# Tokens of a tile laid out by residue modulo 16 in a hybrid attention and gating step

## The chip, the core and the metric

The kernel runs on one core of a Trainium2 chip. Its metric is the device time in microseconds of one launch. A core has five instruction queues that run side by side and meet at semaphores: TensorE (PE in the profile; its weight loads are listed apart as PEld), VectorE (DVE), ScalarE (ACT), GpSimd (POOL) and SyncE (SP), which here only starts transfers. Each queue runs its instructions in program order, so an instruction that waits holds up everything behind it on its engine.

## The reference

One decoder step for a prompt of 2048 tokens and a small sample group (8 sequences of 4 tokens). After a norm and one input projection, eight attention heads of 64 channels and a chunked spatial gate run side by side; their outputs are concatenated, projected, added to the input, and followed by a SwiGLU feed-forward and a last norm. The attention is the part that the change is about: every head evaluates three branches with keys at distances 0, d, 2d, ... up to a window, for (window, d) = (128, 1), (512, 4) and (2048, 16), each with its own softmax, and merges them with weights that come from the softmax denominators.

```python
BRANCHES = ((128, 1), (512, 4), (2048, 16))

def _dilated_prompt(q, k, v, bias_hj, d, nj):
    ...
    s = jnp.einsum('bnqrhc,bnkrhc->bnrhqk', qb, kc).astype(jnp.float32)
    s = s * (HEAD_DIM ** -0.5) + bias[None, None, None]
    s = jnp.where(valid[None, :, None, None], s, NEG_INF)
    lse = jax.nn.logsumexp(s, axis=-1)
    p = jnp.exp(s - lse[..., None])
    o = jnp.einsum('bnrhqk,bnkrhc->bnqrhc', p.astype(vc.dtype), vc)
    ...

def _merge_branches(outs, lses):
    w = jax.nn.softmax(jnp.stack(lses, axis=0), axis=0)
    return jnp.sum(w[..., None] * jnp.stack(outs, axis=0).astype(jnp.float32), axis=0)
```

For d = 16 and 2048 tokens the third branch splits the sequence into 16 residue classes of 128 tokens; within a class it is plain causal attention of 128 queries on 128 keys.

## The kernel before

All matmuls take their operands as pairs of a rounded high part and a low remainder, and add two or three products. The launch has three stages: the projections with the gate and the sample attention (to about 607 us of the profile), the attention heads (607 to about 970 us), and the output projection with the feed-forward (the rest). Projected queries, keys and values go through DRAM (`qk_d`, `v_d`), as does a table of attention biases (`b_d`, written by `table_spread`, L483).

A head is a list of 20 *items* (L1081 to L1084): 16 *band* items, one for each tile of 128 queries, which serve the branches (128, 1) and (512, 4) together on up to five tiles of keys; and four *strided* items ("s"), each with four residue classes of the third branch. In the middle heads (list `OTHER`) the strided items stand at places 2, 7, 12 and 17. Head 0 and head 7 have lists of their own.

The order on each engine is written out by hand. `at(step, phase, function)` files a call, and `Plan.run` issues all calls by step, then by phase (L46: early, exp, low, scores, turn, mid, values, out, misc, store), then in the order of filing. An item at step x passes through these steps:

- x: its scores on PE into a PSUM tile `ps_s` (two buffers), phase scores;
- x + 1: DVE adds the bias and finds the minimum (scores are kept negated); for a strided item POOL then subtracts the minimum (L935);
- x + 2 or x + 3: ACT takes the exponential;
- x + 3 (band) or x + 4 (strided): PE transposes the probabilities into PSUM (`ps_a`, three banks in turn) and ACT copies the high parts out (`ph`, `eh`), phase turn;
- x + 4 in phase low (band) or x + 5 in phase mid (strided): DVE subtracts to get the low parts (`pl`, `el`, L896), after which the bank is free;
- later PE multiplies with the values (L910 for a group of four band items, L958 and L959 for a strided item), and ACT copies the result out (L919 and L966).

`strided_scores` (L921) reads query and key columns with a step of 16 (`bass.ds(r4 * 4 + a, P, step=NT)`), 128 of them, one matmul for each of the two query parts and each of four residues. The queries are the stationary operand, the keys the moving one. `strided_out` (L961) writes the 128 outputs of a residue 16 floats apart, so that `o3` lies in token order.

The class `Stats` (L973) makes the merge weights of a head from minima and sums. Band statistics lie as (token in tile, tile), strided ones as (place in class, class). `a` and `b` bring the band statistics to the strided layout with a small DVE product and two small matmuls (L989); `weights_a` and `weights_b` compute the two factors of each token, and `store` writes them to DRAM (`f_d`), from where `merge_load` spreads them over all partitions for the three operations of `merge` (L1031, on POOL in all heads but the last). For the middle heads the steps of `Stats` are filed at steps 2 to 6 of the next head.

`load_head` (L815) brings a head's queries, keys, biases and values on SP's queue; the values come twice, in tile order for the band (`vb`) and in class order for the strided items (`vp`).

Of the kernel before, what the change touches and what calls it, by code (L numbers as in the profile page):

```python
# [10 lines left out]
F32 = mybir.dt.float32  # L11
# [23 lines left out]
BIG = 3.0e38  # L35
SL = 352


# [26 lines left out]
def hymba_step(ctx: ExitStack, tc: tile.TileContext, A: dict, O: dict):  # L65
# [193 lines left out]
    def gate_loads():  # L259

        mask["w"] = big_raw()
        sync.dma_start(mask["w"], A["sgu_wT"])
        mask["c"] = big_raw()[:, 0]
        sync.dma_start(mask["c"], A["causal"])
        sync.dma_start(sgb, A["sgu_bT"])
        sync.dma_start(lng, dap(A["sgu_ln_g"], 0, [[0, P], [1, DA]]))
        sync.dma_start(lnb, dap(A["sgu_ln_b"], 0, [[0, P], [1, DA]]))
        dve.memset(wbd, 0.0)
        sync.dma_start(sgbs, dap(A["sgu_bT"], 0, [[0, SB], [H, ST], [1, H]]))
        sync.dma_start(cms, A["causal_s"])  # L270

    def gate_diagonal(b):
        sync.dma_start(wbd[b * ST:(b + 1) * ST, :, b * ST:(b + 1) * ST], A["sgu_wT"][0:ST, :, 0:ST])

# [540 lines left out]
    def load_head(h):  # L815

        d = heads[h] = {}
        qk = hev if h % 2 == 0 else hod
        for nm, w_, parts in (("qh", 0, (0, 0)), ("k", 1, (0, 1)), ("ql", 0, (1, 1))):
            t_ = d[nm] = qk.tile([P, T], F32R, name=nm, tag="qk", bufs=3)  # L820

            sync.dma_start(t_.bitcast(F32), dap(qk_d, ((w_ * 2 + parts[0]) * DA + h * C) * T,
                                                [[T, C], [(parts[1] - parts[0]) * DA * T, 2], [1, T]]))
            yield
        b_ = row_tile("b")
        d["b3"], d["b12"] = b_[:, 640:768], b_[:, 0:640]
# [9 lines left out]
        sync.dma_start(t_.bitcast(F32), dap(v_d, h * 2 * C, [[NT * H * 2 * C, P], [H * 2 * C, NT], [1, 2 * C]]))  # L836
# [84 lines left out]
    def strided_scores(it):  # L921
        d, st, r4 = it["d"], it["st"], it["n"]
        it["s"] = s = ps_s()[:, 0, :]
        for a in range(4):
            qs = bass.ds(r4 * 4 + a, P, step=NT)
            pe.matmul(s[:, a * P:(a + 1) * P], d["qh"][:, qs], d["k"][:, qs], start=True, stop=False)
            pe.matmul(s[:, a * P:(a + 1) * P], d["ql"][:, qs], d["k"][:, qs], start=False, stop=True)

# [32 lines left out]
    def strided_out(it):  # L961
        r4, h = it["n"], it["h"]
        if r4 == 0:
            o3s[h] = rp.tile([P, P, NT], F32, name="o3", tag="wide", bufs=2)
        rs = slice(r4 * 4, r4 * 4 + 4)
        act.activation(o3s[h][:, :, rs].rearrange("p i r -> p r i"),  # L966
                       it["o"].rearrange("p (r i) -> p r i", r=4), AF.Copy)

# [4 lines left out]
    class Stats:  # L973
        def __init__(self, h, st, r0=0, r1=P):
            self.h, self.st, self.r0, self.r1 = h, st, r0, r1

        def small(self, tag, n):
            return hsmall(tag, n * NT, 2)[0:self.r1].rearrange("p (a t) -> p a t", a=n)

        def a(self):  # L980
            n = self.r1 // 8
            self.m = ap_.tile([P, 2 * P], F32, name="sm", tag="sm", bufs=1).rearrange("p (a n g) -> p a n g", a=2, g=8)[:, :, 0:n]
            dve.tensor_tensor(self.m, self.st["t"][:, 0:2, 0:n].unsqueeze(3).broadcast_to([P, 2, n, 8]),
                              sel_g.unsqueeze(1).unsqueeze(1).broadcast_to([P, 2, n, 8]), op=OP.mult)

        def b(self):
            self.p = pt = ps_a()
            for z in range(2):
                pe.matmul(pt[0:self.r1, z * NT:(z + 1) * NT], self.m[:, z].rearrange("p n g -> p (n g)"), sel_r, start=True, stop=True)  # L989

        def c(self):
            self.s = self.small("s12", 2)
            dve.tensor_copy(self.s.rearrange("p a t -> p (a t)"), self.p[0:self.r1, 0:2 * NT])

        def weights_a(self):

            m3 = self.st["t"][0:self.r1, 2, :]
            self.f = f = self.small("f", 3)
            dve.tensor_tensor(f[:, 2, :], self.s[:, 0, :], m3, op=OP.min)
            dve.tensor_sub(f[:, 0, :], f[:, 2, :], self.s[:, 0, :])  # L1000
            dve.tensor_sub(f[:, 1, :], f[:, 2, :], m3)
            act.activation(f[:, 0:2, :], f[:, 0:2, :], AF.Exp)

        def weights_b(self):
            f, m = self.f, self.f[:, 2, :]
            dd = self.small("dd", 2)
            dve.tensor_mul(dd[:, 0, :], f[:, 0, :], self.s[:, 1, :])
            dve.tensor_mul(dd[:, 1, :], f[:, 1, :], self.st["t"][0:self.r1, 3, :])
            dve.tensor_add(m, dd[:, 0, :], dd[:, 1, :])
            dve.reciprocal(m, m)  # L1010
            dve.tensor_mul(f[:, 0:2, :], f[:, 0:2, :], m.unsqueeze(1).broadcast_to([self.r1, 2, NT]))
# [19 lines left out]
    def merge(h, ch, eng, part=None):  # L1031
        f1, f3 = mf[h, ch]
        x = obs[h][:, ch * 512:(ch + 1) * 512]
        y = o3s[h].rearrange("p i r -> p (i r)")[:, ch * 512:(ch + 1) * 512]
        if part in (None, 0):
# [66 lines left out]
    for y in (222, 224, 226, 228):  # L1102
        at(y, "misc", load, 0)
    at(232, "misc", load, 0)
    at(B0 + 3, "early", load, 0)
    at(B0 + 3, "store", load, 0)
    for h in range(1, H):
# [3 lines left out]
        for y in (1, 2, 3, 4, 10, 12):  # L1111
            at(s0 + y, "misc", load, h)
    def stats_of(h, steps, r0, r1):
        d = {}
        at(*steps[0], lambda: d.update(s=Stats(h, sts[h], r0, r1)))
        for (y, ph), fn in zip(steps, "a b c weights_a weights_b store".split()):
            at(y, ph, lambda fn=fn: getattr(d["s"], fn)())

    for h in range(H):
# [4 lines left out]
        if end:  # L1124

            x = s0 - NI
            stats_of(h, [(x + y, ph) for y, ph in ((14, "early"), (14, "turn"), (15, "early"), (15, "misc"), (16, "early"), (16, "mid"))], 0, 64)
            steps = ((2, "early"), (2, "turn"), (3, "early"), (4, "early"), (5, "early"), (5, "early"))
            at(x + 18, "mid", merge_load, h, 0)
# [5 lines left out]
        else:  # L1135
            steps = ((2, "misc"), (3, "misc"), (4, "early"), (4, "misc"), (5, "misc"), (6, "mid"))

# [7 lines left out]
            else:  # L1145
                at(s0 + 23, "store", merge_store, h, 0, 4)
        stats_of(h, [(s0 + y, ph) for y, ph in steps], 64 if end else 0, P)
    for i, it in enumerate(items):
# [31 lines left out]

    sel_g = ap_.tile([P, 8], F32, name="sel_g", bufs=1)
    sel_r = ap_.tile([P, NT], F32, name="sel_r", bufs=1)
    dve.reduce_sum(sel_g, ident.rearrange("p (g r) -> p g r", g=8), axis=AX.X)
    dve.reduce_sum(sel_r, ident.rearrange("p (g r) -> p r g", g=8), axis=AX.X)

# [741 lines left out]


def _bucket(dist):
    me = 16  # L1930
# [23 lines left out]
def _shape_constants():  # L1954
# [6 lines left out]
    for t in range(ST):  # L1961
# [3 lines left out]
        for u in range(3):  # L1965
# [6 lines left out]
    headmask = np.repeat((rr[:, None] % H == np.arange(H)[None, :]).astype(np.float32), C, axis=1)  # L1972
    sel = ((rr[:, None] % SR) // H == np.arange(ST)[None, :]).astype(np.float32)
    return {"oh12": oh12, "oh3": oh3, "ohs": ohs.reshape(33, 12, P), "causal": causal, "causal_s": causal_s,
            "headmask": headmask, "sel": sel}
# [6 lines left out]
def _arrays(inp):  # L1982
    f = {k: np.asarray(v) for k, v in inp.items()}
    a = {
        "x_prompt": f["x_prompt"].reshape(T, D),
        "x_promptT": f["x_prompt"].reshape(T, D).T,
        "x_sample": f["x_sample"].reshape(SR, D),
# [6 lines left out]
        "sgu_ln_b": f["sgu_ln_b"],  # L1994
        "sgu_wT": f["sgu_w"][0].transpose(2, 0, 1),
        "sgu_bT": f["sgu_b"][0].T,
        "w_out": f["w_out"][0],
# [29 lines left out]
```

## Time and profile before

| | us |
|---|---|
| three runs: lowest, median, highest | 2689.18, 2700.57, 2710.32 |
| the profiled execution: its span, first to last instruction | 2690.7 |
| projections, gate, sample attention | 0 to about 607 |
| attention heads | about 607 to 970 |
| output projection and feed-forward | about 970 to the end |
| HBM over the span | 382.76 MB read, 165.84 MB written |

The profile gives a span, and no time of its own for what lies around it. In the lines that are shown below, a group's line has the source line, engine, operation, output and inputs by the program's names, shapes and count; after the first bar the total busy time in us and the mean of one in ns; after the second bar the idle time of the engine just before them and what ended it. A line of the order of time has the start in us, the duration in us, and the instruction; idle time before it stands in brackets. Matmuls are pipelined, so the durations of neighbours overlap.

### The profile page before, as it was taken

Reading aid. Unit: us, or ns where it says so; the run is one execution under the profiler, and the core shown is the slowest. Engines: PE = TensorE matmul, PEld = TensorE weight load, DVE = VectorE, ACT = ScalarE, POOL = GpSimd, SP = SyncE. Lnnn points to the kernel's source line nnn. Section 1 sums busy time; section 2 is a strip of 40 time slices with the busy share of each in tenths; the row PEclk is TensorE's granted clock in tenths of the full one; section 3 lists DMA queues with packets and bytes.
Section 4 is the critical chain, followed back from the end, with each engine's and each line's share of the span. In section 5 each row is a group of like instructions: output and inputs, shape, how many; then the busy total and the mean of one; then the engine's idle time right before and its main releaser. Section 6 shows DMA issues by size and latency. Waiting matters only on the chain. (4 is left out here: it accounts for less than half of the span.)

```text
span 2690.7 us, 38857 instructions
## 1 busy us (share of the span) xinstructions
PE 2545.5 (95%) x13578; PEld 2245.5 (83%) x13578; DVE 1423.0 (53%) x2884; ACT 1239.5 (46%) x2617; POOL 1322.9 (49%) x968
## 2 busy tenths in 40 slices
PE   8998899998999979899999999899999998999997
PEld 6777677677888867899899987899999987999996
DVE  3258785436788764444444456444444456444445
ACT  6414344446777654545545444523232335433333
POOL 2036663131444354667677653535454533666663
PEclk9999899998999989899999999999999999999998
DMA  7765844586576565345546366445454454555653
GB/s 244 217 200 160 273 138 144 176 268 219 159 238 170 157 166 188 124 150 178 171 157 196 124 191 199 142 140 196 157 178 170 161 176 139 167 202 200 204 194 119
DMA packets 314680, 481.05 MB, mean 179 GB/s; under 512 B 26968, under 2 KB 179721, under 8 KB 308597
## 3 DMA queue, kind: packets, MB, share of 16 engines
q1 hardware_dynamic: 300100, 455.89, 52.3%
q10 hardware_dynamic: 14384, 22.68, 3.3%
q8 instruction: 108, 1.77, 0.3%
q14 instruction: 88, 0.71, 0.1%
HBM read 382.76 MB, written 165.84 MB: 204 GB/s over the span
## 5 line engine op out<-in xcount | busy, mean ns | idle before, releaser
L1481 POOL TENSOR_TENSOR op<-fr,op 128x512 fp32r<-128x512 f32 x385 | 489.1, 1301 | 302.1 <-ACT op L1477 268.0
L1538 PE MATMUL ps_m<-xh,op 128*128 128x384 f32 (+4 forms) x1932 | 623.4, 323 | 6.4 <-DVE zn L1559 3.0
L1539 PE MATMUL ps_m<-xl,op 128*128 128x384 f32 (+4 forms) x1932 | 621.6, 322 | 0.9 <-DVE xl L1409 0.9
L1540 PE MATMUL ps_m<-xh,op 128*128 128x384 f32 (+4 forms) x1932 | 621.6, 322 | 0.0
L1611 PE MATMUL ps_o<-dw,hw 128*128 128x512 f32 x2040 | 484.1, 392 | 8.2 <-DVE acc L1613 8.2
L1611 PEld LDWEIGHTS ps_o<-dw,hw 128*128 128x128 f32 x2040 | 379.7, 188 | 90.5 <-DVE acc L1613 14.9
L1538 PEld LDWEIGHTS ps_m<-xh,op 128*128 128x128 f32 x1932 | 371.4, 192 | 11.6 <-ACT xh L134 3.8
L1539 PEld LDWEIGHTS ps_m<-xl,op 128*128 128x128 f32 x1932 | 371.7, 192 | 5.4 <-DVE xl L1409 1.3
L1540 PEld LDWEIGHTS ps_m<-xh,op 128*128 128x128 f32 x1932 | 371.2, 192 | 0.0
L1613 DVE TENSOR_TENSOR acc<-acc,ps_o 128x512 f32<-128x512 f32 (+1 forms) x362 | 247.0, 686 | 214.8 <-PE ps_o L1611 214.7
L1578 ACT ACTIVATE ps_t<-zn 128x384 f32<-128x384 f32 (+1 forms) x126 | 58.3, 463 | 477.6 <-DVE zn L1561 371.2
L1477 ACT ACTIVATE op<-fr 128x512 fp32r<-128x512 f32 x396 | 235.5, 622 | 24.5 <-DMA fr<-ab_d 11.7
L137 POOL TENSOR_TENSOR dw<-fd,dw 128x1024 fp32r<-128x1024 f32 x66 | 158.7, 2405 | 122.5 <-ACT dw L134 121.9
L317 PE MATMUL ps_s<-wh,xh 128*128 128x512 f32 x480 | 197.9, 412 | 7.0 <-ACT xh L134 6.1
L318 PE MATMUL ps_s<-wl,xh 128*128 128x512 f32 x480 | 192.2, 400 | 1.4 <-DVE wl L225 1.4
L319 PE MATMUL ps_s<-wh,xl 128*128 128x512 f32 x480 | 191.5, 399 | 0.0
L1481 POOL TENSOR_TENSOR op<-pair,op 128x512 fp32r<-128x512 f32 x63 | 81.4, 1300 | 119.2 <-ACT op L1477 119.2
L1588 ACT ACTIVATE hw<-ps_t 128x384 fp32r<-128x384 f32 (+1 forms) x126 | 56.1, 453 | 176.3 <-DVE ps_t L1584 175.3
L317 PEld LDWEIGHTS ps_s<-wh,xh 128*128 128x128 f32 x480 | 92.8, 193 | 37.2 <-issue 8.4
L935 POOL TENSOR_TENSOR e<-e,st 128x512 f32<-128x512 f32 x32 | 33.3, 1042 | 175.1 <-DVE st L934 124.6
L319 PEld LDWEIGHTS ps_s<-wh,xl 128*128 128x128 f32 x480 | 92.6, 193 | 20.7 <-DVE xl L137 0.3
L318 PEld LDWEIGHTS ps_s<-wl,xh 128*128 128x128 f32 x480 | 93.1, 194 | 20.0 <-DVE wl L225 2.6
(463 smaller groups left out, 4925.9 us busy)
## 6 DMA issues: line engine op xcount, KB each, us to landing
fr<-ab_d SPq DMA_DIRECT2D x308, 256.0 KB
fd<-in_w_down_dram SPq DMA_DIRECT2D x66, 512.0 KB
out_ks_dram<-in_cache_k_dram SPq DMA_DIRECT2D x56, 512.0 KB
out_vs_dram<-in_cache_v_dram SPq DMA_DIRECT2D x56, 512.0 KB
ab_d<-fr SPq DMA_DIRECT2D x88, 256.0 KB
raw<-in_w_in_dram SPq DMA_DIRECT2D x72, 256.0 KB
qk_d<-pair SPq DMA_DIRECT2D x64, 256.0 KB
ab_d<-pair SPq DMA_DIRECT2D x63, 256.0 KB
```

What stands on the lines that cost most here:

```text
L137: (eng_lo or pool).tensor_sub(lo, src, hi.bitcast(F32))
L317: pe.matmul(o[j], xh[:, k, :], wh, start=(k == 0), stop=False)
L318: pe.matmul(o[j], xh[:, k, :], wl, start=False, stop=False)
L319: pe.matmul(o[j], xl[:, k, :], wh, start=False, stop=(k == KD - 1))
L1477: act.activation(ops[f, j][0], ab[f][j], AF.Copy)
L1481: (pool if f or j in POOL_LOW else dve).tensor_sub(lo_, ab[f][j], hi.bitcast(F32))
L1538: pe.matmul(out, wh[:, ks], xh[:, :, k], start=(k == 0), stop=False)
L1539: pe.matmul(out, wh[:, ks], xl[:, :, k], start=False, stop=False)
L1540: pe.matmul(out, wl[:, ks], xh[:, :, k], start=False, stop=(k == 3))
L1578: act.activation(g, c, AF.Silu)
L1611: pe.matmul(ps[0:nr], l_, r_[:, cs], start=(z == 0 and y == 0), stop=(z == FC - 1 and y == len(pairs) - 1))
L1613: dve.tensor_add(B.acc[i][0:nr, cs], B.acc[i][0:nr, cs], ps[0:nr])
```

## The change

Inside every tile of 128 tokens the host puts the tokens in another order: token 16 m + r of the tile (r from 0 to 15, m from 0 to 7) goes to place 8 r + m. The inputs, the causal mask, the gate's weights and biases are permuted alike on the host, and the prompt's outputs are permuted back. In the sequence the eight tokens of a tile that belong to residue class r then stand side by side, and class r is 16 runs of eight with a step of 128.

On the device:

- `strided_scores` reads the keys as 16 runs of eight; the queries come from a contiguous tile `qo`, which `order_queries` fills on POOL, two copies of 128x512 for each strided item, three steps ahead in phase misc.
- The band's bias rows follow the new order by writing the table in eight transfers instead of one (`table_spread`); its columns are reordered for each head by one POOL copy of 128x640 (`order_bias`, step 8 of the head before, phase misc).
- The strided values (`vp`) come in eight transfers of 16 partitions instead of one of 128.
- `strided_out` writes runs of eight floats.
- `Stats` brings the strided statistics to the band's layout instead of the reverse. A new step `turn` transposes the weights on PE, and `store` copies them out of PSUM on ACT before the transfer, which then has rows of 512 bytes. In the last head the two sets are split by tiles instead of by places.
- The sample's part of the gate weights is a small input of its own (`sgu_wsT`).

```diff
+RUN = P // NT
...
     def table_spread():
-        sync.dma_start(b_d[:, :, 0:640], dap(l12_d, 127, [[768, H], [-1, P], [1, 640]]))
+        for m in range(RUN):
+            sync.dma_start(b_d.rearrange("h (r m) c -> m h r c", m=RUN)[m][:, :, 0:640],
+                           dap(l12_d, 127 - m * NT, [[768, H], [-1, NT], [1, 640]]))
...
         t_ = d["vp"] = value_tile(2 * h)
-        sync.dma_start(t_.bitcast(F32), dap(v_d, h * 2 * C, [[NT * H * 2 * C, P], [H * 2 * C, NT], [1, 2 * C]]))
+        R = H * 2 * C
+        for m in range(RUN):
+            sync.dma_start(t_[m::RUN].bitcast(F32), dap(v_d, m * R + h * 2 * C, [[P * R, NT], [RUN * R, NT], [1, 2 * C]]))
...
+    def order_bias(h):
+        d = heads[h]
+        d["b12"] = t_ = (hev if h % 2 == 0 else hod).tile([P, 640], F32, name="bp", tag="bp", bufs=1)
+        pool.tensor_copy(t_.rearrange("p (d r m) -> p d r m", r=NT, m=RUN),
+                         d["b"][:, 0:640].rearrange("p (d m r) -> p d r m", r=NT, m=RUN))
+
+    def by_residue(x):
+        return x.rearrange("p (n r m) -> p r n m", r=NT, m=RUN)
+
+    def order_queries(it):
+        d, r0 = heads[it["h"]], it["n"] * 4
+        it["q"] = t_ = ap_.tile([P, 2, 4, P], F32R, name="qo", tag="qo", bufs=2)
+        for z, q in enumerate(("qh", "ql")):
+            pool.tensor_copy(t_[:, z].rearrange("p r (n m) -> p r n m", m=RUN), by_residue(d[q])[:, r0:r0 + 4])
...
         for a in range(4):
-            qs = bass.ds(r4 * 4 + a, P, step=NT)
-            pe.matmul(s[:, a * P:(a + 1) * P], d["qh"][:, qs], d["k"][:, qs], start=True, stop=False)
-            pe.matmul(s[:, a * P:(a + 1) * P], d["ql"][:, qs], d["k"][:, qs], start=False, stop=True)
+            k = by_residue(d["k"])[:, r4 * 4 + a]
+            out = s[:, a * P:(a + 1) * P].rearrange("p (n m) -> p n m", m=RUN)
+            for z in range(2):
+                pe.matmul(out, it["q"][:, z, a], k, start=(z == 0), stop=(z == 1))
...
-        act.activation(o3s[h][:, :, rs].rearrange("p i r -> p r i"),
-                       it["o"].rearrange("p (r i) -> p r i", r=4), AF.Copy)
+        act.activation(by_residue(o3s[h])[:, rs],
+                       it["o"].rearrange("p (r n m) -> p r n m", r=4, m=RUN), AF.Copy)
...
+        def turn(self):
+            self.p = pt = ps_a()
+            pe.transpose(pt[0:2 * self.n, 0:P], self.w, ident)
+
         def store(self):
-            n = self.r1 - self.r0
-            act.dma_start(dap(f_d, self.h * 2 * T + self.r0 * NT, [[NT, n], [T, 2], [1, NT]]), self.f[self.r0:self.r1, 0:2, :])
+            n = 2 * self.n
+            rows = ap_.tile([2 * NT, P], F32, name="fr", tag="fr", bufs=2)[0:n]
+            act.activation(rows, self.p[0:n, 0:P], AF.Copy)
+            act.dma_start(dap(f_d, self.h * 2 * T + self.n0 * P, [[T, 2], [P, self.n], [1, P]]), rows)
...
+        at(s0 + 8, "misc", order_bias, h)
...
-            steps = ((2, "misc"), (3, "misc"), (4, "early"), (4, "misc"), (5, "misc"), (6, "mid"))
+            steps = ((2, "misc"), (3, "misc"), (4, "early"), (4, "misc"), (5, "misc"), (6, "turn"), (6, "mid"))
...
         if it["kind"] == "s":
+            at(x - 3, "misc", order_queries, it)
...
+    x = _by_residue(f["x_prompt"].reshape(T, D), 0)
...
+    o.update({name: _by_residue(o[name], 0, back=True) for name in ("yp", "kp", "vp")})
```

More of the change, by code (lines that the diff above doesn't have):

```diff
@@ L1112, in hymba_step, with stats_of @@
             at(s0 + y, "misc", load, h)
-    def stats_of(h, steps, r0, r1):
+        at(s0 + 8, "misc", order_bias, h)
+    def stats_of(h, steps, n0, n1):
         d = {}
-        at(*steps[0], lambda: d.update(s=Stats(h, sts[h], r0, r1)))
-        for (y, ph), fn in zip(steps, "a b c weights_a weights_b store".split()):
+        at(*steps[0], lambda: d.update(s=Stats(h, sts[h], n0, n1)))
+        for (y, ph), fn in zip(steps, "a b c weights_a weights_b turn store".split()):
             at(y, ph, lambda fn=fn: getattr(d["s"], fn)())
@@ L1926, in hymba_step, with _by_residue @@
     right.close()
+def _by_residue(a, axis, back=False):
+    s = a.shape
+    two = (NT, RUN) if back else (RUN, NT)
+    a = a.reshape(s[:axis] + (s[axis] // P,) + two + s[axis + 1:])
+    return np.ascontiguousarray(np.swapaxes(a, axis + 1, axis + 2)).reshape(s)
 def _bucket(dist):
```

71 lines of the change are left out of this document (38 added, 33 removed).

## The prediction

> **What bounds the kernel now.** I read the page first, then the busy time by stretches of the attention stage, the groups by line, and last the order of time on three engines around one block of the changed matmuls.
>
> ```profile
> span 2690.7 us, 38857 instructions
> PE 2545.5 (95%) x13578; PEld 2245.5 (83%) x13578; DVE 1423.0 (53%) x2884; ACT 1239.5 (46%) x2617; POOL 1322.9 (49%) x968
> ```
>
> ```profile
> 606.80:969.50 362.70, 330.84 (x2087) 302.27 (x2086) 276.62 (x683) 262.02 (x621) 144.70 (x121) 0.95 0.61 183
> 606.80:648.59 41.79, 35.65 (x206) 32.28 (x204) 28.11 (x67) 26.93 (x66) 6.68 (x6) 0.92 0.70 210
> 915.36:969.50 54.14, 43.72 (x273) 40.09 (x272) 39.24 (x93) 37.08 (x85) 28.06 (x24) 0.91 0.39 106
> 723.12:734.30 11.18, 10.75 (x74) 10.02 (x74) 8.81 (x21) 8.76 (x21) 7.92 (x7) 1.00 0.19 58
> 765.68:778.04 12.36, 12.09 (x74) 11.65 (x74) 8.86 (x21) 8.78 (x21) 8.57 (x7) 0.86 0.24 70
> ```
>
> Columns: stretch and length, then busy us and count of PE, PEld, DVE, ACT and POOL, granted clock, DMA share, GB/s. All that the change speeds up lies in the attention, 606.80 to 969.50: 362.70 us, of which PE is busy 330.84, DVE 276.62, ACT 262.02, POOL 144.70. The second and third rows are heads 0 and 7, the last two are two equal fifths of two later heads. PE looks like the bound, but only by 54 us over DVE, so what PE saves can turn into waiting.
>
> ```profile
> L926 PE MATMUL ps_s<-k,qh 128*128 128x128 f32 x128 | 51.1, 399 | 1.3 <-DVE st L865 1.3
> L927 PE MATMUL ps_s<-k,ql 128*128 128x128 f32 x128 | 50.5, 395 | 0.0
> L966 ACT ACTIVATE o<-ps_o 128x512 f32<-128x512 f32 x32 | 33.7, 1054 | 5.5 <-PE ps_o L959 2.7
> L919 ACT ACTIVATE ob<-ps_o 128x512 f32<-128x512 f32 x32 | 19.0, 595 | 5.9 <-PE ps_o L910 3.2 <-DVE f L1011 2.5
> L935 POOL TENSOR_TENSOR e<-e,st 128x512 f32<-128x512 f32 x32 | 33.3, 1042 | 175.1 <-DVE st L934 124.6 <-PE ps_t L887 16.9 <-DVE s L993 16.9
> ```
>
> There are 256 strided score matmuls, eight in each of 32 blocks. Matmuls overlap, so their price is the distance between starts:
>
> ```profile
> 721.29 0.60 PE L947 MATMUL ps_t<-ident,e 128*128 128x128 f32 x4
> 722.20 0.31 PE L958 MATMUL ps_o<-eh,v 128*128 128x128 f32 x1
> 723.01 0.28 PE L959 MATMUL ps_o<-el,v 128*128 128x128 f32 x1
> 723.12 0.41 PE L926 MATMUL ps_s<-k,qh 128*128 128x128 f32 x1
> 724.65 0.39 PE L927 MATMUL ps_s<-k,ql 128*128 128x128 f32 x1
> 725.32 0.41 PE L887 MATMUL ps_t<-ident,e 128*128 128x128 f32 x2 [0.28 <-DVE el L896]
> 721.93 0.60 ACT L950 ACTIVATE eh<-ps_t 128x512 fp32r<-128x512 f32 x1 [0.22 <-PE ps_t L947]
> 722.42 0.48 ACT L891 ACTIVATE ph<-ps_o 128x384 fp32r<-128x384 f32 x1
> 722.94 0.56 DVE L896 TENSOR_TENSOR pl<-ps_o,ph 128x384 fp32r<-128x384 f32 x1 [1.12 <-ACT ph L891]
> 723.75 0.81 DVE L865 CUSTOM_DVE_ANT_0 e<-ps_s,b 128x640 f32<-128x640 f32 x1
> 724.49 0.69 DVE L896 TENSOR_TENSOR el<-ps_t,eh 128x512 fp32r<-128x512 f32 x1
> ```
>
> This is the view that decides. The eight strided matmuls start from 723.12 to 724.65: 1.53 / 7 = 0.219 us each. The eight value matmuls of the same 128x128 shape with contiguous operands start from 722.20 to 723.01: 0.81 / 7 = 0.116 us each. But the transposes that follow the block start at 725.32, held by DVE's el, which ends at 724.49 + 0.69 = 725.18. That el frees the PSUM bank into which L947, one step earlier, transposed the previous strided item. Its chain is L947 at 721.29, ACT's eh at 721.93, ACT's ph at 722.42, DVE's pl at 722.94, DVE's band bias at 723.75, el. None of these waits for the strided scores: they stand in the shadow of a chain of 725.32 - 721.29 = 4.03 us.
>
> **The change part by part.** *Strided scores.* Stationary queries become contiguous copies, moving keys become runs of eight. If both read like the value matmuls, PE saves 256 x (0.219 - 0.116) = 26.4 us, 0.82 us a block; if the runs of eight still read as slowly as single keys and only the queries gain, about half, 13.2 us. No row shows runs of eight. [...] I take 0.82 us a block.
>
> How much is left after the shadow? In the pattern of the middle heads the four blocks stand at items 2, 7, 12 and 17, five apart, so that each falls one step behind the transposes of the one before.
>
> ```profile
> 704.40 0.74 PE L887 MATMUL ps_t<-ident,e 128*128 128x128 f32 x5
> 703.57 0.69 DVE L896 TENSOR_TENSOR el<-ps_t,eh 128x512 fp32r<-128x512 f32 x1
> 714.73 0.30 PE L887 MATMUL ps_o<-ident,e 128*128 128x128 f32 x1
> 713.90 0.69 DVE L896 TENSOR_TENSOR el<-ps_o,eh 128x512 fp32r<-128x512 f32 x1
> PE ps_t L887 <- DVE el L896: 1.6, 6, 0.3
> PE ps_o L887 <- DVE el L896: 1.1, 4, 0.3
> PE ps_s L859 <- DVE st L865: 6.4, 15, 1.5
> ```
>
> The last three are the only waits of PE from 699 to 916, heads 2 to 6. Items 12 and 17 of these five heads make the 6 + 4 recorded waits on el. At item 2 (el ends 704.26, transposes start 704.40) and item 7 (el ends 714.59, the transpose into the freed bank starts 714.73) PE also starts 0.14 us after el, the same distance as 725.18 to 725.32: there it is just balanced now. So in all four positions a shorter block buys idle time before the same start. I put the direct gain of heads 1 to 6 at nothing.
>
> Blocks without an el behind them: three in head 0, the first of head 1 and the four of head 7, 8 x 0.82 = 6.6 us. In heads 0 and 7 PE is already idle 41.79 - 35.65 = 6.1 us and 54.14 - 43.72 = 10.4 us, waiting on others, so I take half: **3.3 us gained** (bounds 0 and 6.6).
>
> *The strided output copy on ACT (L966).* It writes one float every 64 bytes for 1054 ns; the contiguous copy L919 takes 595. With runs of eight I take 0.6, 32 x 0.459 = 14.7 us less ACT. In the quoted loop it runs behind ph and is not a link of the chain to el. At item 7 it stands before the first ph and lets DVE's work be earlier by up to its 0.45 us, which can shorten the waits on L865, 6.4 / 5 = 1.3 us a head. I take 0.4 for six heads: **2.4 us gained** (bounds 0 and 7.7).
>
> *Merge weights (class Stats).* The two small gather matmuls and DVE's small operations stay, on the other branch's numbers. New for 9 sets: a PE transpose, an ACT copy of it, and a contiguous store.
>
> ```profile
> 710.87 0.19 DVE L1011 TENSOR_TENSOR f<-f 128x32 f32<-128x32 f32 x1
> 710.91 0.60 PE L947 MATMUL ps_o<-ident,e 128*128 128x128 f32 x4
> ```
>
> The new transpose stands on PE just ahead of L947, the head of the chain above. Its input ends at 711.06; with the 0.14 us of hand-over and 0.116 of its own, L947 starts 0.4 us later, with everything of PE queued behind it. 7 x 0.4, plus 0.5 for each of the two last-head sets: **3.8 us lost** (bounds: 9 x 0.116 = 1.0 if DVE is early, 8 if the copy also delays ph). The ACT copy of 32x128 comes after ph and before the output copy, which gets shorter by more than it costs.
>
> *POOL.* 64 query copies of 128x512 and 8 bias reorderings of 128x640. POOL has 362.7 - 144.7 = 218 us free. No POOL copy is in the trace: bounds are nothing and the 2.4 us of a two-input operation on 128x1024; I take 1.04 from L935, one full operand, 64 x 1.04 = 67 us plus some 10. It matters when the pair is ready, since PE's strided scores wait for it and all of PE stands behind them.
>
> ```profile
> L137 POOL TENSOR_TENSOR dw<-fd,dw 128x1024 fp32r<-128x1024 f32 x66 | 158.7, 2405 | 122.5 <-ACT dw L134 121.9 <-DMA fr<-ab_d 0.6
> 784.76 1.30 POOL L1038 TENSOR_TENSOR o<-o,pair 128x512 f32<-128x512 f32 x1
> 794.20 1.04 POOL L935 TENSOR_TENSOR e<-e,st 128x512 f32<-128x512 f32 x1 [2.94 <-DVE s L993]
> 788.95 0.41 PE L926 MATMUL ps_s<-k,qh 128*128 128x128 f32 x1
> ```
>
> The tightest pair stands behind the merge that ends at 786.06 and is needed at 788.95: 2.9 us for two copies, 2.1 needed. The merges behind it run 2.1 later, but POOL then idled 2.94 before its next urgent operation at 794.20. Cost taken: **0**; without that cover up to 2 us a block.
>
> *Transfers.* The strided values come by eight DMAs a head instead of one, with the same bytes; SP issued the one in 0.57 us:
>
> ```profile
> L836 SPq DMA_DIRECT2D v<-v_d x8: 540/568/604, 620.5 to 884.2; - x8
> ```
>
> At that price it is 4 us more a head on a queue behind which only the other value load and a store wait, and the values are needed more than ten items later. The bias table's spread also becomes eight DMAs, once, in the projection stage. Both 0; if the first were late, a few us. Inputs and outputs permuted on the host cost the device nothing.
>
> Sum: -3.3 - 2.4 + 3.8 = -1.9 us. The profiled span, 2690.7, lies near the fastest of the three runs (2689.18) and 9.9 us under their median of 2700.57; no row shows what lies around the span, so I take the difference to the median: 2700.57 - 1.9 = **2698.7 us**.
>
> **Rivals.** *A, the saving comes through* (el arrives earlier or the order slips so that other waits stop holding). For it: PE is busy 91% of the stage. Time: -26.4 - 2.4 + 3.8 = -25, 2676 us; with all of ACT's 14.7 as well, 2661. Against it: ten recorded waits and ten balanced starts.
>
> *B, POOL late.* It decides from about 1.8 us a copy: 2.9 us of cover plus the 0.82 by which the block gets shorter is 3.7 for two. At 2.4 each the pair is 4.8 - 2.9 = 1.9 late, less 0.82 is 1.1 us; times 32 is 35 us: 2735. L935 at 1042 ns speaks against it.
>
> *C, PE's clock.* The stretch from 765.68 is the same work as that from 723.12, but at a clock of 0.86 instead of 1.00 and 1.2 us longer. The change replaces slow work by idle time in the same place. If one block in four set off such a stretch, 8 x 1.2 = 10 us, 2709; every block, 38 us, 2737. [...]
>
> *D, the runs of eight are as slow as single keys*: 13.2 instead of 26.4 on PE, and in the shadow no difference; it is within the forecast.
>
> **How the numbers follow.** Forecast with D 0.60, A 0.16, B 0.11, C 0.13. The forecast alone spans 2690 to 2708, its bounds and the scatter of runs. For 8 in 10 I add half of A and the lower half of B and C: 2680 to 2718. A measurement of this kernel can tell about 1% (27 us) from no change. Under 2673.6: the upper part of A, 0.07. Over 2727.6: half of B and the far part of C, 0.11. Between: 0.82.
>
> **What would show it.** Right: blocks of strided scores that take about 0.9 us for eight starts, and PE's waits on el at L887 grown from 0.3 to above 1 us in nearly all blocks of heads 1 to 6, the stage near 361 us. Wrong: a stage of 340 us with small waits on el (A); strided scores waiting on POOL's copies (B); a stage clock well under 0.95 (C); block starts still 0.16 to 0.2 us apart (D).

## The result, and the profile after

The changed kernel takes 2717.28 us (median of nine runs, 2707.5 to 2725.7) against 2704.67 us for the kernel before on the same chips. The ratio is 1.0062, with a 95% interval of 1.0038 to 1.0086: 0.6% slower. On the 2700.57 us from which the prediction started that is 17 us more, where 1.9 us less had been forecast.

The profiled execution took 2724.02 us (span 2722.2), at the upper end of its runs, while that of the kernel before was at the lower end of its own. So the spans (31.5 us apart) overstate the difference, and I compare stretches. The one that counts runs from the first band scores (607.00 us before, 608.14 after) to the first matmul of the feed-forward, and holds the attention and the output projection. Its end is the first time in these rows of the two kernels (one line's instructions: shortest, median and longest in ns, then from when to when):

```profile
L1538 PE MATMUL ps_m<-xh,op x63: 273/415/628, 1077.4 to 1120.0; 128*128 128x256 f32 x28, 128*128 128x128 f32 x28, 128*128 128x384 f32 x7
```

```profile
L1572 PE MATMUL ps_m<-xh,op x49: 273/281/562, 1092.9 to 1119.9; 128*128 128x256 f32 x28, 128*128 128x128 f32 x21
```

That is 470.4 us before and 484.8 after, 14.4 more. Of the rest of the spans' difference 1.1 us lies ahead of it and 16.0 behind it, where no line of the kernel was changed.

Busy time by stretches, the changed kernel: head 0, and one later head with the clock at 1.00 throughout. A later head is taken from one of DVE's `sm` products (the small product in `Stats`, one a head) to the next. Columns as in the prediction.

```profile
608.14:661.89 53.75, 33.15 (x204) 29.02 (x203) 28.68 (x69) 26.58 (x66) 13.48 (x17) 0.81 0.66 163
763.10:806.50 43.40, 37.49 (x267) 33.69 (x267) 35.42 (x88) 31.60 (x79) 24.99 (x26) 1.00 0.69 209
```

The kernel before, such a later head:

```profile
704.20:746.75 42.55, 40.58 (x268) 36.86 (x267) 34.35 (x89) 32.59 (x78) 18.57 (x16) 1.00 0.69 200
```

Head 0 grew from 41.59 us (607.00 to 648.59; the prediction's row starts 0.2 us earlier) to 53.75. In a later head PE works 3.1 us less (37.49 for 40.58), and yet the head is 0.85 us longer; DVE works 1.1 us more. Heads come with the clock at 1.00 or, about half of them, with a short stretch of lower clock and some 1.2 us longer; below, heads at 1.00 are compared. These are one clean head of each kernel. The mean of heads 2 to 5, with the low clock left in, is 43.46 us before and 44.44 after. The loss is not the same in every head: one of the four in the kernel before takes 43.72 us at full clock, with a wait of 1.53 us on `st`.

The groups by line of the changed kernel, attention only:

```profile
L950 PE MATMUL ps_s<-k,qo 128*128 128x128 f32 x256 | 36.7, 290 | 15.3 <-POOL qo L865 14.5 <-DVE st L887 0.7
...
L989 ACT ACTIVATE o<-ps_o 128x512 f32<-128x512 f32 x32 | 19.2, 601 | 7.0 <-PE ps_o L982 4.8
L854 POOL COPY bp<-b 128x640 f32<-128x640 f32 x7 | 9.2, 1307 | 21.4 <-DMA b<-b_d 21.4
```

All that was to become faster did: the 256 strided matmuls are busy 36.7 us instead of 101.6, ACT's output copy takes 601 ns instead of 1054. A block of eight strided matmuls takes 1.06 to 1.09 us from its first start to its last end at full clock; before it was 1.92 (723.12 to 725.04 in the prediction's lines). A query copy takes 0.62 us. The two long waits in the right-hand column are new.

What PE waits for in the attention, first before, then after (us in total, times, longest):

```profile
PE ps_t L887 <- DVE el L896: 9.8, 12, 3.0
PE ps_s L859 <- DVE st L865: 8.8, 21, 1.5
PE ps_o L887 <- DVE el L896: 4.8, 6, 2.3
```

```profile
PE ps_t L909 <- DVE el L918: 19.8, 18, 2.6
PE ps_s L950 <- POOL qo L865: 14.5, 1, 14.5
PE ps_o L909 <- DVE el L918: 13.9, 10, 3.1
PE ps_s L881 <- DVE st L887: 13.2, 27, 0.9
```

Waits on `el` went from 14.6 to 33.7 us: as forecast, time saved on the strided scores became waiting on `el`. In heads 2 to 6 alone, 713.35 to 934.49 us, the changed kernel has

```profile
PE ps_t L909 <- DVE el L918: 12.7, 14, 1.2
PE ps_o L909 <- DVE el L918: 6.0, 6, 1.1
```

where the prediction's rows had 1.6 and 1.1 us: 16.0 us more, and the 20 strided blocks of these heads save 16.4 at the prediction's 0.82 each.

The second row of the changed kernel was not forecast: one wait of 14.5 us. Its place, in order of time on POOL, PE and SP of the changed kernel, with rows left out:

```profile
635.37 1.25 POOL L854 COPY bp<-b 128x640 f32<-128x640 f32 x1 [21.43 <-DMA b<-b_d]
636.57 0.62 POOL L865 CAST qo<-qh 128x512 fp32r<-128x512 f32 x1
637.13 0.62 POOL L865 CAST qo<-ql 128x512 fp32r<-128x512 f32 x1
...
637.24 2.31 PE L950 MATMUL ps_s<-k,qo 128*128 128x128 f32 x8 [14.54 <-POOL qo L865]
...
620.79 0.37 SPq L836 DMA_DIRECT2D ve<-v_d  x1
621.80 6.77 SPq L841 DMA_DIRECT2D v<-v_d  x8
628.83 0.39 SPq L830 DMA_DIRECT2D b<-b_d  x1
```

In the middle of head 0, POOL reaches `order_bias` of head 1, which needs head 1's bias rows `b`. SP issues that load only at 628.83: it stood still until the value load at 620.79, 7.5 us of that because stores of `v_d` had not landed, and then the eight transfers of `vp` took it 6.77 us. POOL waits 21.43 us, and the query copies for a strided item of head 0 stand behind in its queue. PE needs them and waits 14.54 us, with everything behind it. In the kernel before nothing read `b` of head 1 until head 1 began, and SP had it issued sooner:

```profile
620.46 0.60 SPq L836 DMA_DIRECT2D v<-v_d  x1
621.11 4.28 SPq L827 DMA_DIRECT2D b<-b_d  x1
```

The stall costs more than its own length. Right behind it PE's granted clock is 0.50, and the first block takes 2.31 us where one at full clock takes 1.06:

```profile
637.20:641.60 4.40, 4.27 (x14) 3.70 (x15) 1.97 (x3) 2.26 (x5) 2.73 (x5) 0.50 1.22 225
```

### The profile page after: what moved, and what is told of

Its sections match the earlier page's. It is cut to its first block, busy times and chain, and to the rows that moved or that the text cites. A ratio compares the mean times of both kernels' runs of the same rounds, so it can differ in the third digit from the quotient of the medians.

```text
span 2722.2 us, 39058 instructions
## 1 busy us (share of the span) xinstructions
PE 2530.3 (93%) x13587; PEld 2228.3 (82%) x13587; DVE 1425.4 (52%) x2884; ACT 1232.1 (45%) x2626; POOL 1366.8 (50%) x1040
```

## The experiments

Three questions: is that stall the loss; why does PE's saved time not come through; and where do the later heads lose 0.85 us each, though PE works less?

**The stall.** Head 1's bias copy six steps later:

```diff
-        at(s0 + 8, "misc", order_bias, h)
+        at(s0 + (14 if h == 1 else 8), "misc", order_bias, h)
```

> The bias copy of head 1 on POOL is filed at step 14 of head 0 instead of step 8; nothing else differs from the changed kernel. Theory S (the stall: in head 0 this copy waits 21.4 us for the transfer of b, and the query copies behind it on POOL hold the strided scores for 14.5 us): the 14.5 us wait is gone, head 0 falls from 53.75 us to about 42 (41.8 before), and the time falls by about 12 us against the changed kernel's median of 2717.3, to 2705 (ratio to the kernel before 1.000 to 1.003). Rival M (the loss is spread over the middle heads, which are 0.8 to 1.5 us longer each by the two profiles, and over the clock): the wait moves to another transfer of head 0, the time falls by less than 5 us, to 2713 or more.

Measured: 2699.24 us, ratio 0.9994 (0.9968 to 1.002). The 14.5 us wait is gone; the longest wait left on `qo` is 0.7 us. Head 0:

```profile
608.91:648.07 39.16, 30.77 (x204) 27.40 (x203) 28.58 (x69) 26.74 (x66) 13.51 (x17) 0.96 0.87 222
```

It takes 39.16 us, where 42 were expected. One re-filed call returns 18 us, by the medians and by the two ratios, and the changed kernel is level with the one before. Theory S holds, with a gain larger than the 12 us expected; M falls. In the two profiles the stretch to the feed-forward is 15.0 us shorter, and 14.6 of them are head 0.

The other way to break it: the load ahead of the eight transfers, the copy where it was.

```diff
-        for y in (1, 2, 3, 4, 10, 12):
+        for y in (1, 2, 3, 3 if h == 1 else 4, 10, 12):
             at(s0 + y, "misc", load, h)
```

> The transfer of b for head 1 is issued on SP ahead of the eight strided value transfers of head 0 instead of behind them; the copy on POOL stays at step 8. Theory S1 (what makes b late is that it stands behind the eight value transfers, 6.8 us of issue and their bytes): the copy starts at about 625 to 627 us of the profile instead of 635.4, the strided scores wait 3 to 6 us instead of 14.5, and the time falls by 8 to 11 us, to about 2708. Rival S2 (b is late for what holds the queue before, the stores and the value load until 620.8): b lands hardly earlier and less than 4 us is gained.

Measured: 2708.79 us, ratio 1.0039 (1.0016 to 1.0062). POOL, in order of time:

```profile
629.08 1.25 POOL L854 COPY bp<-b 128x640 f32<-128x640 f32 x1 [16.29 <-DMA b<-b_d]
```

and PE's wait on `qo` is 9.4 us. Some half of the loss comes from standing behind the eight transfers; the copy is 2 us later than expected, and the other half remains: `b` is late for what holds SP before them as well. What is shown is that in head 0 the copy at step 8 is too early for this load in both of the orders tried.

**The chain through `el`.** DVE's `el` is filed ahead of the band bias of its step instead of behind it:

```diff
-            at(x + 5, "mid", low_parts, it)
+            at(x + 5, "scores", low_parts, it)
```

> In the changed kernel DVE's el is filed ahead of the band bias of the same step instead of behind it; nothing else differs. Theory H: el ends about 0.9 us earlier, PE's 33.7 us of waits on el fall to under 12, the part that comes through is what the later bias (0.89 us with its read) does not give back through scores that wait for it: 5 to 20 us gained, 2697 to 2712, with the 14.5 us stall of head 0 still there. Rival N (the loop through DVE is as long either way): PE's waits on el turn into waits on the band's minimum st, the time stays within 4 us of 2717.

Measured: 2698.11 us, ratio 0.999 (0.9965 to 1.0015), 19 us below the changed kernel although the stall, 18.6 us in its profile, is still there. Waits of PE, and a later head:

```profile
PE ps_s L950 <- POOL qo L865: 18.6, 1, 18.6
PE ps_s L881 <- DVE st L887: 16.3, 35, 1.0
PE ps_t L909 <- DVE el L918: 6.3, 13, 1.5
PE ps_o L909 <- DVE el L918: 3.6, 8, 1.0
```

```profile
717.80:759.30 41.50, 37.84 (x268) 33.73 (x269) 35.34 (x88) 31.40 (x79) 24.96 (x26) 1.00 0.75 204
```

Waits on `el` fall from 33.7 to 9.9 us, those on `st` rise by 3, and the head falls from 43.40 to 41.50 us. The place of `el` in DVE's queue held the time back. The same edit in the kernel before, the control:

> The kernel before with el ahead of the band bias of its step, and nothing else. Theory H (in the kernel before PE is nearly busy throughout, and el holds it for 0.3 us at a time; only the faster strided scores leave idle time that an earlier el can give back): 0 to 1 us a head, an undisturbed head at 41.7 to 42.5, the time at 2695 to 2702. Rival (the order on DVE is a gain by itself, whatever the layout): about 19 us as in the changed kernel, 2683, and heads at 41.6 or less.

Measured: 2689.31 us, ratio 0.9964 (0.9942 to 0.9985), a later head at 41.70:

```profile
746.00:787.70 41.70, 40.17 (x268) 36.98 (x268) 35.02 (x90) 32.69 (x78) 19.39 (x17) 1.00 0.68 218
```

Between the two theories: the order is worth 10 us by itself, 0.85 us a head at full clock, and 19 us in the changed kernel, 1.9 us a head. So some 9 of the 19 us come out of the change's saving, and the rest the same order gives the kernel before as well. I had put the first at 0 to 1 us a head but the time at 2695 or more; the time is 6 us lower.

Six heads at these sizes make only 5 of the 10 us and 11 of the 19. The rest goes with the clock: in the 14 profiles heads 2 to 5 show a stretch of low clock (a mean of 0.93 or 0.96 over the head) in 22 of 40 cases with `el` behind the band bias, and in 1 of 16 with `el` ahead of it. With the low clock left in, the mean of these heads falls from 43.46 to 42.00 us in the kernel before and from 44.44 to 41.63 in the changed one. Why the clock holds there, no run shows.

Both edits in the changed kernel:

> The two edits together: the bias copy of head 1 at step 14 of head 0, and DVE's el ahead of the band bias of its step. Alone the first gave 2699.2 us, the second 2698.1, the changed kernel 2717.3. If they are independent (one removes the stall of head 0, the other lets the PE time that was saved come through in the later heads), the gains of 18 and 19 us add up: 2680 us, ratio to the kernel before 0.990 to 0.994, and the stretch from the first band scores to the first matmul of the feed-forward falls from 470 us to about 455. If the earlier el only fed on time that the stall had made idle, the two together give no more than one alone, 2695 or more.

Measured: 2678.77 us, ratio 0.9922 (0.9903 to 0.994); the stretch from the first band scores to the feed-forward is 446.5 us, shorter than the 455 expected. The gains add up: this version beats both kernels, and the earlier `el` fed on more than the stall's idle time.

**Which operand was dear.** The keys read with a step of 16 floats again, the queries contiguous:

```diff
-            k = by_residue(d["k"])[:, r4 * 4 + a]
+            k = d["k"][:, bass.ds(r4 * 4 + a, P, step=NT)]
```

> The strided scores read their keys again with a step of 16 floats (the keys of other tokens, so the third branch is computed on a wrong choice of keys), with contiguous queries as in the changed kernel. Theory H (what PE saves is hidden in the chain that ends with el): the eight starts of a block take longer than the 1.06 to 1.09 us of the changed kernel, up to 1.53, PE's waits on el in the middle heads fall by as much, and the time stays within 4 us of 2717. Rival A (the saving comes through): if the block grows by 0.4 us, 32 x 0.4 = 13 us more, 2730. The block's own time also tells which operand set the price: near 1.53 us the moving keys, near 1.07 the stationary queries.

Measured: 2719.24 us, ratio 1.0061 (1.003 to 1.0093), level with the changed kernel. PE's strided block (the line is one higher up here) and then all its weight loads:

```profile
785.70 1.09 PE L949 MATMUL ps_s<-k,qo 128*128 128x128 f32 x8
```

```profile
L949 PEld LDWEIGHTS ps_s<-k,qo 128*128 128x128 f32 x256 | 33.8, 205 | 19.2 <-POOL qo L865 18.2 <-issue 1.0
```

The block takes 1.09 us, as with keys in runs of eight. (The 1.53 us of the expectation run from the first start to the eighth; the figure of the kernel before that compares with 1.09 is 1.92.) So the run tells nothing of what is hidden, since it made nothing slower; it does tell that the moving operand's step costs nothing here, and that all of PE's saving comes from the query copies. The kernel before shows it from the other side, in its weight loads:

```profile
L927 PEld LDWEIGHTS ps_s<-k,ql 128*128 128x128 f32 x128 | 39.7, 311 | 0.0
```

311 ns in the mean with strided queries, 205 with contiguous ones.

**The 0.85 us of a later head.** All that follow but one build on the kernel with the late bias copy (2699.24 us). A later head of it at full clock takes as long as one of the changed kernel:

```profile
748.10:791.45 43.35, 37.46 (x267) 33.68 (x267) 35.36 (x89) 31.59 (x79) 24.92 (x26) 1.00 0.71 210
```

The expectations of the first three speak of the mean of heads 2 to 5, 44.35 us here with one of the four at full clock. That number differs from execution to execution, so I go by heads at full clock, and give the mean beside them. First without the transpose of the merge weights:

```diff
         def turn(self):
-            self.p = pt = ps_a()
-            pe.transpose(pt[0:2 * self.n, 0:P], self.w, ident)
+            pass
...
-            act.activation(rows, self.p[0:n, 0:P], AF.Copy)
+            act.activation(rows, ident[0:n, 0:P], AF.Copy)
```

> The changed kernel with the bias copy of head 1 at step 14, without the PE transpose of the merge weights and without the PSUM bank that it takes (the weights stored for the merge are constants). Heads 2 to 5 take 44.35 us each in the kernel with the late bias copy and 43.46 in the kernel before. Theory T (the transpose on PE and its bank, priced at 0.4 us a head in the prediction, make up the 0.9): heads 2 to 5 at 43.5 or less. Rival F (they are longer because ACT waits for DVE's f, 7.3 us in five heads instead of 3.3): heads 2 to 5 stay at 44 or more. In time 3 to 7 us are at stake.

Measured: 2695.05 us, ratio 0.9994 (0.9977 to 1.001). A later head:

```profile
708.70:751.80 43.10, 37.22 (x266) 33.61 (x266) 35.40 (x88) 31.57 (x79) 24.95 (x26) 1.00 0.70 200
```

43.10: the transpose costs about 0.25 us a head, not 0.9. The mean of heads 2 to 5, 43.17, would fit theory T, but here all four are at full clock; and the ratio is the 0.9994 of the kernel with the transpose. Then ACT's exponential of `f` one step later:

```diff
+        def weights_e(self):
+            f = self.f
             act.activation(f[:, 0:2, :], f[:, 0:2, :], AF.Exp)
...
-            steps = ((2, "misc"), (3, "misc"), (4, "early"), (4, "misc"), (5, "misc"), (6, "turn"), (6, "mid"))
+            steps = ((2, "misc"), (3, "misc"), (4, "early"), (4, "misc"), (5, "mid"), (5, "misc"), (6, "turn"), (6, "mid"))
...
```

> The changed kernel with the bias copy of head 1 at step 14, and ACT's exponential of the merge weights' f filed one step later, behind ph of step 5, where DVE has long written f. Theory F: ACT's waits on f fall from 7.3 us in five heads to under 1.5, and heads 2 to 5 from 44.35 us to about 43.5. Theory T (the transpose of the weights): ACT's waits are gone and heads 2 to 5 stay within 0.3 of 44.35.

Measured: 2702.71 us, ratio 1.0001 (0.9984 to 1.0019). ACT's waits on `f` are gone from the later heads, and a head at full clock takes 43.40 as before (the mean is 43.76, with three of four at full clock): theory F falls; ACT's wait on `f` costs nothing that these runs can tell. Then the slow output copy:

```diff
-        act.activation(by_residue(o3s[h])[:, rs],
-                       it["o"].rearrange("p (r n m) -> p r n m", r=4, m=RUN), AF.Copy)
+        act.activation(o3s[h].rearrange("p (i r) -> p i r", r=NT)[:, :, rs].rearrange("p i r -> p r i"),
+                       it["o"].rearrange("p (r i) -> p r i", r=4), AF.Copy)
```

> The changed kernel with the bias copy of head 1 at step 14, and the strided output copy writing one float every 64 bytes again (so the third branch is merged at wrong tokens). It tests the term of 2.4 us that the prediction gave to the faster copy (bounds 0 and 7.7). ACT's copy of 128x512 takes about 1.05 us instead of 0.60. Right: 1 to 4 us slower than 2699.2, heads 2 to 5 about 0.4 longer each and PE's waits on st larger. Wrong at 0: heads 2 to 5 within 0.2 us of 44.35. Wrong at the upper end: 0.7 us or more a head.

Measured: 2706.04 us, ratio 1.0013 (0.9992 to 1.0034), not separable in time from the kernel with the late bias copy. A later head:

```profile
701.70:745.40 43.70, 37.78 (x267) 33.64 (x267) 35.38 (x88) 32.94 (x80) 25.00 (x26) 1.00 0.75 198
```

43.70 for 43.35: 0.35 a head, near the 0.4 that the prediction gave to the faster copy. The mean, 44.33, hides it, with two of four at full clock. PE's waits on `st` did not grow, so it doesn't come by the way named there; by which way, no run shows.

What remained was DVE's extra microsecond. The kernel with the late bias copy, in order of time on DVE and POOL:

```profile
752.29 0.55 DVE L1023 TENSOR_TENSOR f<-st,s 128x16 f32<-128x16 f32 x1
752.88 0.52 DVE L1024 TENSOR_TENSOR f<-f,st 128x16 f32<-128x16 f32 x1
753.32 0.63 DVE L1025 TENSOR_TENSOR f<-f,s 128x16 f32<-128x16 f32 x1
...
751.77 1.04 POOL L958 TENSOR_TENSOR e<-e,st 128x512 f32<-128x512 f32 x1 [1.92 <-DVE s L1017]
752.76 0.61 POOL L865 CAST qo<-qh 128x512 fp32r<-128x512 f32 x1
753.31 0.61 POOL L865 CAST qo<-ql 128x512 fp32r<-128x512 f32 x1
```

Each of the three small DVE operations ends 0.03 us after the POOL operation that runs beside it: 752.84 and 752.81, 753.40 and 753.37, 753.95 and 753.92. In the kernel before POOL is idle at the second and third:

```profile
708.96 0.17 DVE L1000 TENSOR_TENSOR f<-f,s 128x16 f32<-128x16 f32 x1
709.06 0.17 DVE L1001 TENSOR_TENSOR f<-f,st 128x16 f32<-128x16 f32 x1
```

So the copies were moved away, to step 2:

```diff
-            at(x - 3, "misc", order_queries, it)
+            at(x - (5 if n == 1 and 0 < h < H - 1 else 3), "misc", order_queries, it)
```

> The changed kernel with the bias copy of head 1 at step 14, and in heads 1 to 6 the query copies of the second strided item filed on POOL at step 2 instead of step 4 of the head. In an undisturbed head DVE is busy 35.4 us instead of 34.4 in the kernel before, and 0.8 of that are two subtractions of the merge weights (128x16) that take 0.52 and 0.63 us instead of 0.17 each, while POOL runs the two query copies. Theory P (DVE's operations with two SBUF inputs stand still while POOL runs a copy): with the copies out of the way both take about 0.17 us, an undisturbed head falls from 43.36 us to about 42.6, and the time by 4 to 6 us, to about 2694. Rival O (they are slow for their own operands): they stay at 0.5 to 0.6, the heads at 43.3, the time at 2699.

Measured: 2696.86 us, ratio 0.9986 (0.9965 to 1.0007). DVE, and a later head:

```profile
752.03 0.17 DVE L1024 TENSOR_TENSOR f<-f,st 128x16 f32<-128x16 f32 x1
752.12 0.17 DVE L1025 TENSOR_TENSOR f<-f,s 128x16 f32<-128x16 f32 x1
```

```profile
747.30:789.80 42.50, 37.31 (x267) 33.63 (x267) 34.59 (x89) 31.61 (x79) 23.98 (x24) 1.00 0.71 203
```

Both subtractions are back at 0.17 us, DVE's work at 34.6 us and the head at 42.50, where the kernel before has it. The mean of heads 2 to 5 falls from 44.35 to 43.58 us. In time the 2.4 us are within the intervals, where 4 to 6 were expected, and the stretch to the feed-forward is no shorter in this profile (471.2 us for 469.8). And the reverse, the kernel before with the copies added at `at(x - 3, "misc", order_queries, it)` and read by nothing:

> The kernel before, with the 64 query copies on POOL added at the places where the changed kernel has them; nothing reads them. Theory P: L1000 and L1001 of the kernel before, 0.17 us each in the middle heads, go to 0.5 or 0.6, an undisturbed head from 42.5 to 43.2 or 43.3 us, the time 4 to 6 us up, 2705 to 2708. Rival (POOL's copies cost nothing, as the prediction had it): heads at 42.5, the time within 2 us of 2702.

Measured: 2708.36 us, ratio 1.0025 (1.0007 to 1.0042). A later head, and its DVE:

```profile
704.10:747.50 43.40, 40.83 (x268) 37.01 (x268) 35.43 (x88) 32.62 (x78) 23.79 (x25) 1.00 0.69 200
```

```profile
752.30 0.52 DVE L1007 TENSOR_TENSOR f<-f,s 128x16 f32<-128x16 f32 x1
752.74 0.63 DVE L1008 TENSOR_TENSOR f<-f,st 128x16 f32<-128x16 f32 x1
```

POOL's copies alone make a later head of the kernel before as long as one of the changed kernel, 43.40 us. For these two subtractions the runs show theory P in both directions: 0.52 and 0.63 us beside POOL's copies, 0.17 without them. The parts of a later head add up: 0.85 us lost to POOL's copies and 0.25 to the transpose, less 0.35 for the output copy, make 0.75, where 42.55 grew to 43.35.

All three edits together:

> The three edits together: bias copy of head 1 at step 14, el ahead of the band bias, query copies of the second strided item at step 2. The first two gave 2678.8 us. If the DVE time won from POOL's copies is on the path of a head there too: 0.5 to 0.8 us off each of heads 1 to 6, 2673 to 2676. If the earlier el has already taken it off the path: 2677 to 2680.

Measured: 2684.79 us, ratio 0.9934 (0.9909 to 0.9959). A later head takes 40.70 us, the shortest of all:

```profile
746.00:786.70 40.70, 37.75 (x269) 33.77 (x269) 34.55 (x90) 31.56 (x79) 25.11 (x26) 1.00 0.77 227
```

The time doesn't show it: 2684.79 us is above both expectations, and the interval overlaps that of the version with two edits. In the profiles of the two versions, one execution of each, heads 3 to 6 are 2.8 us shorter together with the third edit, but the stretch from the first band scores to the first `sm` product is 4.9 us longer (53.84 for 48.97), at a clock of 0.85 for 0.97, and this edit leaves head 0 alone. PE waits 4.5 us there for a `vp` transfer that has not landed, and in the version with two edits it stands 3.1 us at the same place. What took the gain stays open.

## Why the prediction was right and wrong

*What failed* is the part on transfers: "4 us more a head on a queue behind which only the other value load and a store wait ... Both 0". In head 0 the load of `b` for head 1 stands behind the eight, and the change gives `b` a reader on POOL that comes far sooner than the old one. The part on POOL failed with it: it counted POOL's busy time and the cover of its tightest pair, and not what the instruction ahead in POOL's queue waits for. The issue, priced at 4 us more a head, was 6.77 us instead of 0.60 in head 0. With the one copy re-filed the ratio is 0.9994, that is 1.6 us less than before (8.6 less to 5.4 more); the sum had said 1.9 less. That nearness is luck in part, since two things that the sum did not have cancel in it: POOL's cost in the later heads, and a larger gain in the others. That 2717.28 us lies within the stated 2680 to 2718 is luck as well, since the range was widened for rivals whose mechanisms are not what happened. "If the first were late, a few us" named the queue, but not who waits, and was far too small. The price of the eight was too low in the later heads as well: from the first issue to the end of the last they take 5.1 to 14.6 us a head in the changed kernel, but there no wait of PE on a transfer follows from it.

*POOL, cost 0* was also wrong in the later heads: 0.85 us each, on DVE. The reasons given (a copy at 1.04 us, cover of 2.9) were on the safe side, 0.62 was measured; rival B's price was never near. B's sign, strided scores that wait on POOL's copies, did appear in head 0, but for the bias load ahead of them and not for their own length. In the later heads the path was another: beside POOL's copies two small operations of DVE take 0.52 and 0.63 us instead of 0.17.

*Strided scores, 0.82 us a block*: right. A block fell from 1.92 to 1.09 us, and PE's work in a later head by 3.1 us (four blocks: 3.3). That keys in runs of eight were needed for it, and read like contiguous ones, was my estimate, which no row of the kernel before shows; the runs show that the keys did not matter: 1.09 us a block with runs of eight and with single keys.

*The shadow, nothing gained in heads 1 to 6*: right. In heads 2 to 6 waits on `el` took up 16.0 us where 16.4 were saved, four waits a head. The sign had been waits above 1 us in nearly all blocks; two of the four are 1.1 to 1.2 us long, the other two 0.7. With the earlier `el` they shrink and time comes out. The chain was read rightly; whether DVE's order in it could be turned was not asked, and that alone is worth 10 us in the kernel before.

*Blocks without an `el` behind them, 3.3 us gained.* With the late bias copy the attention stretch, from 608.9 to 1078.7 in its profile, is 469.8 us against 470.4. Heads 2 to 5 lose about 0.9 each there, so the other heads together gain about 4 us, 2.4 of them in head 0. One execution of each: in line with the forecast, no more.

*Output copy, 2.4 us gained*: 0.35 us a head where 0.4 was taken. *Merge weights, 3.8 lost*: 0.25 us a head instead of 0.4. Both small, both near; the first came by another way than the waits on L865.

*Rivals.* A did not happen in the changed kernel and does, in part, with the earlier `el`: the version with both edits took 2678.77 us, A had said 2676, but some 10 us of that gain the same order gives the kernel before. (A's 2661 counts the 2.4 us of the output copy twice; without that it is 2663.) C is not needed for the loss of a later head, which a head at full clock shows whole; that idle time at a block sets off a stretch of low clock was my estimate, and was not shown. The clock does take part elsewhere: it is 0.50 right behind the stall, and with the earlier `el` a low stretch shows in 1 of 16 heads instead of 22 of 40. D falls: a block takes 1.09 us with keys in runs of eight and with single keys.

## What to carry to other kernels

When a change puts a new reader on an in-order engine, price the moment at which its input lands, not only its duration: the load was timed for the old reader, and all that stood behind the waiting instruction waited too (21.43 us on POOL, and through it 14.54 on PE). Time saved on an engine that sits in a loop may show up only when the next link of the loop moves as well: here 16.0 of 16.4 us became waiting, until one DVE operation was filed a few places earlier. Work given to an engine that seems idle can still cost (here 0.85 us a head, on DVE): look at what its neighbour does at the same time.

## What the runs showed of the hardware

- Two 128x16 subtractions on DVE took 0.52 and 0.63 us where POOL ran a copy beside them, and 0.17 each where it did not, in the kernel before and in the changed one. With the minimum ahead of them (0.55 us, beside a POOL subtraction) each of them ended 0.03 us after the POOL operation beside it. By which way POOL holds them up, no run shows.
- Of the strided scores' two operands only the stationary one made a difference here: with queries 64 bytes apart a weight load took 311 ns in the mean, with contiguous ones 205. With contiguous queries a block of eight matmuls took 1.09 us, whether its keys lay 64 bytes apart or in runs of eight.
- POOL's copy from float32 to fp32r of 128x512 took 0.62 us, well under the 1.04 of its subtraction of the same size.
- Eight transfers of 16 partitions instead of one of 128 took SP 6.77 us in head 0, and 5.1 to 14.6 us over the heads of the changed kernel, from the first issue to the end of the last. The one took 0.54 to 0.60 us.
- After 14.54 us without a matmul PE ran at a granted clock of 0.50 for the next 4.4 us, and a block of 1.06 us took 2.31.
